# Output projection of the mixer as seven block products, its inputs as blocks and sums of blocks, the result read back for the query projection

## The chip, the cores and the metric

One Trainium2 chip, one of its cores. A core has a matrix engine (PE, with its weight loads PEld), a vector engine (DVE), an activation engine (ACT), GpSimd (POOL) and SyncE (SP); each works through its own list of instructions in order. Transfers between DRAM and SBUF are issued here by SP and, for the caches of the decode rows, by POOL. The metric is the time of one execution in microseconds, the median of three runs.

## The reference

One step of a one-layer decoder on 512 prompt tokens and 8 decode tokens, 520 columns in all, with a model width of 2048. Cut to what matters here:

```python
y = jnp.concatenate([y_rnn, y_ml], axis=-1).astype(h.dtype) @ w['w_out']   # mixer
x = x + y.astype(x.dtype)
q = (rmsnorm(x, w['g_xattn']) @ w['w_cq'])                                 # cross attention
...
x = x + o @ w['w_co']
x = x + (jnp.square(jax.nn.relu(hf @ w['w_up'])) @ w['w_down'])
```

The product with `w_out` is 2048 x 2048 by 2048 x 520. Its inputs come from two head groups: rows 0 to 1023 of `y` from the RG-LRU group after a norm over all of them, rows 1024 to 2047 from the mLSTM group, each gated by a sigmoid of a column block of `z`.

## The kernel before

Activations lie transposed: a tile has 128 rows of the model width and 520 columns, in two halves of 260. Every float32 product is made of three: a value is cast to a shorter "hi" part (ACT) and the rest is "lo" (DVE), and hi·hi, hi·lo and lo·hi are summed in PSUM. So each matmul takes one 128 x 128 block of weights and 260 columns.

All weight products are a list of jobs, one for each 512 KB of weights (8 blocks of 128 x 128). `run_jobs` issues, for each job, the loads of weights three and four jobs ahead, and the cast and the subtraction of the weights two jobs ahead (`w_split`, L128 and L129; rings of three buffers for `wraw`, `whi` and `wlo`), then a step of every background task (generators in `tasks`), then the job's matmuls, then its `post`, which evicts PSUM. The jobs from the tenth to the middle of the query projection are put in order by the framework's scheduler, by priority and dependencies; the order of what follows is the order of the code.

The stages that the change touches:

- The gate columns of `w_in`, eight products of two jobs each (`ev_og`, L778 to L780): eviction with a scale (DVE), sigmoid (ACT), product (DVE), then a split into `ymh` and `yml` (L230, L231). Beside them the last RG-LRU blocks are scaled (L768) and split into `yrh`, `yrl`. PSUM has two `mm` tiles, so the eviction of one product frees the tile for the product after next.
- `w_out` (`residual`): 16 output blocks, each a plain product of two jobs and 96 matmuls at L202. The residual input comes from `xT` into `xr`; L803 adds it; the sum `x1` is stored to the DRAM tile `dx` (L804) for the later `w_co` stage and at once split into `xah`, `xal` (L233, L234) for the query projection; its squares are summed in `ssx` (L264, L265).
- `w_cq`: 16 products of `xatt` (the splits), with the root of `ssx` applied at the eviction.
- The caches of the decode rows stream through a pool `kv` of 14 tiles of 512 columns, loaded by POOL: one tile for each half of K or V of one decode row, and one for the query or probability rows.

Further on the kernel has the seven-product form already: `quad_jobs` (L1253 for its matmuls) takes a 2 x 2 arrangement of weight blocks A11, A12, A21, A22 and seven products P1 to P7 of 24 matmuls each; four combinations of weights (S3, S1, S2 and S2's successor) are made on DVE at L1223. The activations come as eight blocks, of which 1, 2 and 3 are plain halves and 4 to 7 are differences. The up projection uses it for 31 of 32 column groups and the down projection for all. Before the up projection the differences for six of the eight pairs of rows go through DRAM (`td`) and two are kept (`fact_out`, `sums_out`, `fact_sums`), while the first column group is a plain product (`up_plain`).

Of the kernel before, what the change touches and what calls it, by code (L numbers as in the profile page):

```python
# [17 lines left out]
P = 128  # L18
# [27 lines left out]
def tile_trunk(ctx: ExitStack, tc: tile.TileContext, a, o):  # L46
# [27 lines left out]
    def stream(shape):  # L74
        return small.tile(list(shape), F32, tag="kv", name=nm("kv"), bufs=14)
# [232 lines left out]
    xact, y = [], []  # L308
# [213 lines left out]
    def ml_decode(h, q, k, hh):  # L522
# [28 lines left out]
        def fetch(b2):  # L551
            qb, ct = [], []
            for b in (2 * b2, 2 * b2 + 1):
                t = stream((P, 512))
                stream_load(t, rows_of(dqk, b * 512, 512))
                qb.append(t)
            for j in range(2):
                t = slot("ct", (P, 2, 256))
                stream_load(t, a["C0"][h, j, :, 2 * b2:2 * b2 + 2])
                ct.append(t)  # L560
            return qb, ct

        ahead = [fetch(0), fetch(1)]
        for b2 in range(NB // 2):
            yield
            qb, ct = ahead.pop(0)
            if b2 + 2 < NB // 2:
                ahead.append(fetch(b2 + 2))
            for j in range(2):
                for i in range(2):  # L570
                    b = 2 * b2 + i
                    c = ct[j][:, i]
                    S.activation(c, c, AF.Copy, scale=bc[:, h, 0, b:b + 1])
                    V.scalar_tensor_tensor(out=c, in0=qb[i][:, 256:512], scalar=gv[:, j, b:b + 1],
                                           in1=c, op0=ALU.mult, op1=ALU.add)
                    junk = sm("junk", (P, 256), 1)
                    V.tensor_tensor_reduce(out=junk, in0=c, in1=qb[i][:, 0:256], op0=ALU.mult,
                                           op1=ALU.add, scale=1.0, scalar=0.0,
                                           accum_out=numd[:, j, b:b + 1])
                load(o["s_C"][h, j, :, 2 * b2:2 * b2 + 2], ct[j])  # L580
# [138 lines left out]
    def rnn(i, xc):  # L719
# [41 lines left out]
        if i == 7:  # L761
# [3 lines left out]
            for i in range(8):  # L765
# [4 lines left out]
                y.append(split(hg[i], "yr"))  # L770


    ym = []

    def ev_og(i):
        def ev(ps):
# [39 lines left out]
    xatt, oact = [], []  # L816
# [32 lines left out]
    def attn_decode_all():  # L849
# [4 lines left out]
        got, scs, dps, pbs = [], {}, {}, {}  # L854

        def fetch(n):
# [3 lines left out]
            ts = [stream((P, 512)) for _ in range(2)]  # L860
            for i in range(2):
                if kind == "K":
                    stream_load(ts[i], a["K"][h, b, i])
                else:
                    stream_load(ts[i].rearrange("p (a b) -> p a b", a=2), a["V"][h, b, i])
            if kind == "K":
                t = stream((P, 512))
                stream_load(t, rows_of(dq_[h], b * 512, 512))
            elif b % 2 == 0:
                t = stream((P, 2, NMEM))  # L870
                stream_load(t, rows_of(dps[h], b * NMEM, 2 * NMEM).rearrange("p (a b) -> p a b", a=2))
                pbs[h] = t
            else:
                t = pbs[h]
# [5 lines left out]
        for n, (kind, h, b) in enumerate(order):  # L880
# [9 lines left out]
            if kind == "K":  # L890
                if b == 0:
                    scs[h] = sm("sc", (P, 2, NB))
                for i in range(2):
                    V.tensor_tensor_reduce(out=ts[i], in0=ts[i], in1=row, op0=ALU.mult, op1=ALU.add,
# [3 lines left out]
            else:  # L898
                for j in range(4):
                    t = ts[j // 2][:, (j % 2) * NMEM:(j % 2 + 1) * NMEM]  # L900
                    V.tensor_tensor_reduce(out=t, in0=t, in1=row[:, b % 2], op0=ALU.mult, op1=ALU.add,
# [222 lines left out]
    def pair_slot(name):  # L1124
        return slot(name, (P, 2, HT), F32R)

    def split_to(out, src, g=None):

        hi, lo = out[:, 0], out[:, 1]
        if g is None:  # L1130
            S.copy(hi, src)
            V.tensor_tensor(out=lo, in0=src, in1=hi.bitcast(F32), op=ALU.subtract)
        else:
            S.activation(hi, src, AF.Copy, scale=g)
            V.scalar_tensor_tensor(out=lo, in0=src, scalar=g, in1=hi.bitcast(F32),
                                   op0=ALU.mult, op1=ALU.subtract)

# [7 lines left out]
    NKEPT = 2  # L1145
# [5 lines left out]
    def fact_out(x1, n):  # L1151
# [10 lines left out]
        if kp:  # L1162
            S.activation(r[:, 2:4], halves(x1), AF.Copy, scale=pc(C_FFN, n))
            block_sums(r)
            if i < len(td):
                start(sums_out(tkept.pop(i), i))
        else:
# [12 lines left out]
    def fact_sums():  # L1180

        n = len(td)
        for i in range(KB // 2):
            tact[i][1], tact[i][2], tact[i][3] = fact[2 * i][0], fact[2 * i + 1][0], fact[2 * i + 1][1]

        def fetch(j, some):
            for i in some:
                tact[i][j] = pair_slot("ta")
                load(tact[i][j].bitcast(F32), td[i][j - 4])
        for i in range(n, KB // 2):  # L1190
            fetch(6, range((i - n) * n // NKEPT, (i - n + 1) * n // NKEPT))
            for j in (6, 4, 5, 7):
                tact[i][j] = pair_slot("ta")
                split_to(tact[i][j], tkept[i][:, j])
            del tkept[i]
            yield
        for j in (4, 5, 7):
            fetch(j, range(n // 2))
            yield
            fetch(j, range(n // 2, n))  # L1200
            yield

    def quad_jobs(srcs, acts, nacc, evac, order=None):
# [4 lines left out]
        def raw2(name, src=None):  # L1208
            t = late["sb"].tile([P, 8, P], F32, tag="wq", name=nm(name), bufs=5)
# [30 lines left out]
        def mm(p, wh, wl):  # L1240
            acc = ACC[p]
            if acc not in ps:
                ps[acc] = mm_tile()
# [40 lines left out]

    def up_plain(i):
# [3 lines left out]
        def mm(mp, kp, wh, wl):  # L1289
            if kp == 0:  # L1290
                box["ps"] = mm_tile()
            ps = box["ps"]
            for j in range(8):
                x = fact[2 * j + kp]
                for wi, (w, b) in enumerate(((wh, 0), (wh, 1), (wl, 0))):
                    for hf in range(2):
                        PE.matmul(ps[:, hf, 0:HT], w[:, j, :], x[hf][:, b],  # L1297
                                  start=(kp == 0 and j == 0 and wi == 0), stop=(kp == 1 and j == 7 and wi == 2))

        def post(mp):  # L1300
# [3 lines left out]
            for hf in range(2):  # L1304
                blk = (1 - hf, 2 + hf)[mp]
                V.scalar_tensor_tensor(out=r[:, blk], in0=box["ps"][:, hf, 0:HT], scalar=0.0,
                                       in1=st["rssf"][:, HALF[hf]], op0=ALU.max, op1=ALU.mult)
            if mp:
                start(hidden(r, i))

        js = []
        for mp in range(2):
            for kp in range(2):
                js.append(dict(src=a["w_up"][i, mp, kp], mm=lambda wh, wl, mp=mp, kp=kp: mm(mp, kp, wh, wl)))
            js[-1]["post"] = lambda mp=mp: post(mp)
        return js

# [163 lines left out]
    jobs += residual("w_co", oact, dx[0], dx[1], "ssf", fact_out, lambda: start(fact_sums(), 2.0))  # L1481
# [34 lines left out]
def _pack(i):  # L1516
# [10 lines left out]
    for base, name in ((C_MIX, "g_mix"), (C_X, "g_xattn"), (C_FFN, "g_ffn"), (C_FIN, "g_final"),  # L1527
# [33 lines left out]
        w_out=gran(i["w_out"][0]), w_cq=gran(i["w_cq"][0]), w_co=gran(i["w_co"][0]),  # L1561
# [50 lines left out]
```

## Time and profile before

| what | value |
|---|---|
| median of three runs | 2691.73 us (2691.72 to 2692.03) |
| the profiled execution's own time | 2690.68 us |
| its span from first to last instruction | 2688.8 us |
| busy: PE, DVE, ACT, POOL | 2663.4, 2053.1, 1220.3, 152.0 us |
| PE in the `w_out` stage, 589 to 772 us | busy 183.0 of 183.0 us |
| DVE and ACT in the same stretch | busy 70.3 and 52.1 us |

The span is what the trace covers; the execution's own time has 1.9 us more around it. Engine times are busy times. Matmuls overlap, so the mean duration of one is not its cost: the cost is the distance between their starts.

### The profile page before, as it was taken

What the parts mean: (1) busy time and instruction counts of PE and PEld (TensorE: products, weight loads), DVE (VectorE), ACT (ScalarE), POOL (GpSimd) and SP (SyncE); (2) the same over time, 40 slices, a digit from 0 to 9 for tenths busy, and PEclk for the clock granted to TensorE, in tenths of its full rate; (3) what the DMA queues carried; (4) which work ended last, traced back from release to release, by engine and by line L of the source; (5) the groups of instructions that cost most, each with busy time, mean ns of one, the idle gap of its engine ahead of it and who ended that gap; (6) DMA issues with size and microseconds to landing.
All of it is one profiled execution on the core that took longest, in us unless ns stands there. A gap on an engine that the chain in (4) does not pass through costs nothing.

```text
span 2688.8 us, 52718 instructions
## 1 busy us (share of the span) xinstructions
PE 2663.4 (99%) x21586; PEld 2628.4 (98%) x21586; DVE 2053.1 (76%) x3447; ACT 1220.3 (45%) x1653; POOL 152.0 (6%) x288
## 2 busy tenths in 40 slices
PE   9999999999999999999999999999999999999997
PEld 9999999999999998989999999999999999999997
DVE  6786686853345567775469999999999898898898
ACT  5646355542233135444345555555554333333344
POOL 0011010000001322210000000000000000000001
PEclk9999999999999999999999999999999999999999
DMA  5354353524436787876566656556569666555642
GB/s 203 105 189 138 119 168 105 170 95 139 138 126 200 261 271 259 276 249 195 184 213 218 218 190 211 192 192 211 191 223 336 233 215 225 170 165 206 206 134 88
DMA packets 225923, 512.41 MB, mean 191 GB/s; under 512 B 25502, under 2 KB 91710, under 8 KB 225682
## 3 DMA queue, kind: packets, MB, share of 16 engines
q1 hardware_dynamic: 205074, 441.92, 49.3%
q0 software_dynamic: 20608, 67.13, 7.6%
q8 instruction: 170, 2.79, 0.4%
q14 instruction: 71, 0.58, 0.1%
HBM read 416.16 MB, written 92.94 MB: 189 GB/s over the span
## 4 chain that ended last, share of the span: by engine, by line
PE 92%; issue 4%; DVE 2%; DMA 1%; ACT 1%; POOL 0%; SPq 0%; POOLq 0%; DVEq 0%; ACTq 0%
PE mm L1253 44%; PE mm L202 35%; PE mm L982 3%; PE mm L1013 3%; PE aux L221 3%; PE mm L1297 1%; DMA out_rh<-hs 1%; DVE wlo L129 0%; PE aux L729 0%; PE aux L658 0%; DMA wraw<-in_w_in 0%; PE aux L662 0%; ACT whi L128 0%; DMA wraw<-in_w_mv 0%; PE aux L655 0%
## 5 line engine op out<-in xcount | busy, mean ns | idle before, releaser
L128 ACT CAST whi<-wraw 128x1024 fp32r<-128x1024 f32 x396 | 416.0, 1050 | 810.0 <-PE mm L1253 369.8
L1253 PE MATMUL mm<-ha,whi 128*128 128x260 f32 x3584 | 644.3, 283 | 1.5 <-ACT whi L128 1.0
L129 DVE TENSOR_TENSOR wlo<-wraw,whi 128x1024 fp32r<-128x1024 f32 x396 | 484.1, 1222 | 203.4 <-ACT whi L128 201.4
L1253 PEld LDWEIGHTS mm<-ha,whi 128*128 128x128 f32 x3584 | 551.4, 188 | 2.4 <-ACT whi L128 1.2
L1253 PE MATMUL mm<-ha,wlo 128*128 128x260 f32 x1792 | 505.4, 282 | 0.5 <-DVE wlo L129 0.5
L1253 PE MATMUL mm<-ta,whi 128*128 128x260 f32 x1984 | 358.4, 282 | 0.0
L1253 PEld LDWEIGHTS mm<-ha,wlo 128*128 128x128 f32 x1792 | 337.0, 188 | 1.0 <-DVE wlo L129 0.9
L1253 PEld LDWEIGHTS mm<-ta,whi 128*128 128x128 f32 x1984 | 305.4, 188 | 0.0
L1253 PE MATMUL mm<-ta,wlo 128*128 128x260 f32 x992 | 279.9, 282 | 0.0
L1253 PE MATMUL mm<-fa,whi 128*128 128x260 f32 x1488 | 270.9, 283 | 0.0
L202 PE MATMUL mm<-xh,whi 128*128 128x260 f32 x1280 | 263.9, 287 | 0.0
L202 PE MATMUL mm<-xl,whi 128*128 128x260 f32 x1280 | 259.4, 283 | 0.0
L202 PE MATMUL mm<-xh,wlo 128*128 128x260 f32 x1280 | 257.2, 282 | 0.0
L1253 PEld LDWEIGHTS mm<-fa,whi 128*128 128x128 f32 x1488 | 229.2, 188 | 0.0
L137 ACT CAST whi<-wraw 128x1024 fp32r<-128x1024 f32 x100 | 105.0, 1050 | 251.8 <-PE mm L202 92.4
L128 ACT CAST whi<-A 128x1024 fp32r<-128x1024 f32 x126 | 132.2, 1049 | 187.2 <-PE mm L1253 133.5
L1253 PE MATMUL mm<-fa,wlo 128*128 128x260 f32 x744 | 210.2, 283 | 0.0
L1362 DVE TENSOR_TENSOR X<-mm,X 128x260 f32<-128x260 f32 x448 | 170.9, 422 | 41.0 <-PE mm L1253 40.1
L202 PEld LDWEIGHTS mm<-xh,whi 128*128 128x128 f32 x1280 | 198.2, 188 | 1.2
L202 PEld LDWEIGHTS mm<-xh,wlo 128*128 128x128 f32 x1280 | 198.0, 189 | 0.2
L202 PEld LDWEIGHTS mm<-xl,whi 128*128 128x128 f32 x1280 | 197.7, 189 | 0.3
L1253 PEld LDWEIGHTS mm<-ta,wlo 128*128 128x128 f32 x992 | 186.9, 188 | 0.0
(397 smaller groups left out, 5246.5 us busy)
## 6 DMA issues: line engine op xcount, KB each, us to landing
ha<-hc SPq DMA_DIRECT2D x224, 260.0 KB, 5.3
wraw<-in_w_in SPq DMA_DIRECT2D x80, 512.0 KB, 4.2
wraw<-in_w_up SPq DMA_DIRECT2D x66, 512.0 KB, 5.6
wraw<-in_w_down SPq DMA_DIRECT2D x64, 512.0 KB, 4.2
A<-in_w_down SPq DMA_DIRECT2D x64, 512.0 KB, 5.6
A<-in_w_up SPq DMA_DIRECT2D x62, 512.0 KB, 5.7
hc<-hhi SPq DMA_DIRECT2D x32, 910.0 KB, 4.3
hc<-r SPq DMA_DIRECT2D x32, 910.0 KB
```

The costliest lines, as they stand in the source:

```text
L128: S.copy(hi, raw)
L129: V.tensor_tensor(out=lo, in0=raw, in1=hi.bitcast(F32), op=ALU.subtract)
L137: S.copy(hi, raw)
L202: PE.matmul(ps[:, hf, 0:HT], w[:, j, :], x[:, HALF[hf]], start=(k == 0 and wi == 0), stop=(k == n - 1 and wi == 2))
L221: PE.matmul(out, u, v, start=first and i == 0, stop=last and i == 2)
L982: PE.matmul(box["ps"], w[:, i, :], x, start=(k == 0 and wi == 0), stop=(k == KB - 1 and wi == 2))
L1013: PE.matmul(box["ps"][:, i], x[:, ms], w[:, j], start=(k == 0 and wi == 0), stop=(k == KB - 1 and wi == 2))
L1253: PE.matmul(out, w[:, j, :], x[:, b], start=(new and k == 0 and wi == 0), stop=(p == LAST[acc] and k == per - 1 and wi == 2), skip_group_c ...
L1297: PE.matmul(ps[:, hf, 0:HT], w[:, j, :], x[hf][:, b], start=(kp == 0 and j == 0 and wi == 0), stop=(kp == 1 and j == 7 and wi == 2))
L1362: V.tensor_tensor(out=x, in0=c, in1=x, op=ALU.add)
```

## The change

`w_out` becomes one plain group of two output blocks (`out_plain`, four jobs, 192 matmuls) and seven groups of seven products (`out_quad`, 49 jobs, 168 matmuls a group), by the same `quad_jobs` as further on, with its weights in the `kv` pool and its partial sums in `mm` and `aux` tiles of PSUM. Its inputs are split in halves (`y_out`), and for each pair of rows four differences are made on DVE (`y_sums`); six pairs go to DRAM as hi and lo and come back as 24 tiles `ta` (`block_loads`), two pairs are kept. Inputs and differences hold so many of the 66 `slots` that `x1` is no longer split as it is made: blocks 0 to 13 are stored to `dx` and, during the last group, read back and split (`x1_again`); blocks 14 and 15 are split directly. The `kv` pool becomes 7 tiles of 1024 columns, and each transfer of the decode caches has twice the size. `w_out` is laid out in blocks in the input array.

```diff
     def stream(shape):
-        return small.tile(list(shape), F32, tag="kv", name=nm("kv"), bufs=14)
+        return small.tile(list(shape), F32, tag="kv", name=nm("kv"), bufs=7)
...
-                y.append(split(hg[i], "yr"))
+                y_out(hg[i], i)
...
-            ym.append(split(hm[i], "ym"))
+            y_out(hm[i], 8 + i)
             if i == 7:
-                assert not tasks and len(y) == 8
-                y.extend(ym)
+                start(block_loads(ty, fy, ydram, ykept), 2.0)
...
+    def y_out(t, n):
+        fy[n] = [pair_slot("fy") for _ in range(2)]
+        for hf in range(2):
+            split_to(fy[n][hf], t[:, HALF[hf]])
+        if n % 2 == 0:
+            y_even[n // 2] = t
+        else:
+            start(y_sums(n // 2, y_even.pop(n // 2), t))
+
+    def y_sums(i, t0, t1):
+        yield
+        r = stream((P, 4, HT))
+        b12, b11, b21, b22 = t0[:, HALF[1]], t0[:, HALF[0]], t1[:, HALF[0]], t1[:, HALF[1]]
+        for k, p, q in ((0, b12, b11), (2, b22, r[:, 0]), (1, b22, b12), (3, b21, r[:, 2])):
+            V.tensor_tensor(out=r[:, k], in0=p, in1=q, op=ALU.subtract)
+        if i >= len(ydram):
+            ykept[i] = {j: r[:, j - 4] for j in range(4, 8)}
+            return
+        yield
+        hi = small.tile([P, 4, HT], F32R, tag="kv", name=nm("kv"), bufs=7)
+        S.copy(hi, r)
+        V.tensor_tensor(out=r.bitcast(F32R), in0=r, in1=hi.bitcast(F32), op=ALU.subtract)
+        for b, x in enumerate((hi.bitcast(F32), r)):
+            load(ydram[i][:, :, b].rearrange("j p c -> p j c"), x)
...
+    def x1_load(m):
+        for n in (2 * m, 2 * m + 1):
+            x1[n] = slot("x1") if m else xr_tile()
+            load(x1[n], a["xT"][n])
+
+    def x1_done(n):
+        load(dx[0][n], x1[n])
...
+        add_sq(st["ssx"], x1[n], n == 0)
...
+        if n >= KB - 2:
+            xatt[n] = split(x1[n], "xa", pc(C_X, n))
+
+    def x1_again():
+        raw = {}
+        for n in range(0, KB, 2):
+            for k in (n, n + 1):
+                if k < KB - 2:
+                    raw[k] = slot("x1")
+                    load(raw[k], dx[0][k])
+            if n:
+                for k in (n - 2, n - 1):
+                    xatt[k] = split(raw.pop(k), "xa", pc(C_X, k))
+            yield
+
+    def out_plain():
+        def post(mp, ps):
+            V.tensor_tensor(out=halves(x1[mp]), in0=ps[:, :, 0:HT], in1=halves(x1[mp]), op=ALU.add)
+            x1_done(mp)
+            if mp:
+                x1_load(1)
+        js = plain_pair(a["w_out"][0], fy, post)
+        js[0]["pre"] = lambda: x1_load(0)
+        js[1], js[2] = js[2], js[1]
         return js
+
+    def out_quad(m):
+        def evac(p, ps):
+            n, hf = dict(P1=(0, 0), P2=(0, 0), P6=(0, 1), P5=(1, 1), P7=(1, 1), P3=(0, 1), P4=(1, 0))[p]
+            x = x1[2 * m + n][:, HALF[hf]]
+            V.tensor_tensor(out=x, in0=ps[:, 0, 0:HT], in1=x, op=ALU.add)
+            if p == "P5" and m + 1 < KB // 2:
+                x1_load(m + 1)
+            if p in ("P3", "P4"):
+                x1_done(2 * m + n)
+            if p == "P4" and m == KB // 2 - 2:
+                start(x1_again())
...
-    jobs += residual("w_out", y, [a["xT"][n] for n in range(KB)], dx[0], "ssx",
-                     lambda x1, n: xatt.append(split(x1, "xa", pc(C_X, n))))
+    jobs += out_plain()
+    for m in range(1, KB // 2):
+        jobs += out_quad(m)
```

`block_loads` is the old `fact_sums` with its arguments passed in, and waits until a kept pair is there; `plain_pair` is the body of the old `up_plain`; `quad_jobs` gets `early=True`, which takes the tiles of weights from `kv` and the partial sums y and z from `aux`.

In the compiled program PE's list is the same before and after the `w_out` stage, but for line numbers. Three places where the lists change follow. First DVE, in the gate products: the rows around the eviction of the fifth of the eight products (`og_6877<-mm_6764` before, `og_6905<-mm_6773` now; `wlo` are weights two jobs ahead, `kv_6847` and `kv_6852` the differences of two pairs of rows). Before:

```order
L129 TENSOR_TENSOR wlo_6888<-wraw_6748,whi_6887 128x1024
L231 TENSOR_TENSOR yml_6745<-hh_2792,ymh_6744 128x520
L231 TENSOR_TENSOR yrl_6756<-hs_4509,yrh_6755 128x520
L231 TENSOR_TENSOR yrl_6761<-hs_4975,yrh_6760 128x520
L231 TENSOR_TENSOR yrl_6821<-hs_5933,yrh_6820 128x520
L231 TENSOR_TENSOR yrl_6826<-hs_6392,yrh_6825 128x520
L778 TENSOR_TENSOR og_6877<-mm_6764,rssq_722 128x520
```

and now:

```order
L819 TENSOR_TENSOR kv_6847<-hs_3541,hs_3083 128x260
L819 TENSOR_TENSOR kv_6847<-hs_3541,kv_6847 128x260
L819 TENSOR_TENSOR kv_6852<-hh_2789 128x260
L819 TENSOR_TENSOR kv_6852<-hh_2790,hh_2789 128x260
L798 TENSOR_TENSOR fy_6830<-hs_5915,fy_6830 128x260
L798 TENSOR_TENSOR fy_6836<-hs_6368,fy_6836 128x260
L819 TENSOR_TENSOR kv_6852<-hh_2790,kv_6852 128x260
L130 TENSOR_TENSOR wlo_6988<-wraw_6822,whi_6987 128x1024
L798 TENSOR_TENSOR fy_6837<-hs_6368,fy_6837 128x260
L819 TENSOR_TENSOR kv_6852<-hh_2790,kv_6852 128x260
L826 TENSOR_TENSOR kv_6847<-kv_6847,kv_6921 128x1040
L775 TENSOR_TENSOR og_6905<-mm_6773,rssq_728 128x520
```

Between the last sum of the RG-LRU squares (`ssr`) and this eviction DVE's list had 43 rows and now has 73: one `wlo` more (7 for 6), 22 subtractions of 128x260 for the splits in the place of 11 of 128x520, 15 differences of 128x260 and 3 subtractions of 128x1040; the other rows are the same.

Second SP, where the plain group ends and the first group of seven begins. Before, the residual input of a block (`xr`) was loaded two blocks ahead of its use, behind the store of an earlier block:

```order
L804 DMA dx_0_103<-x_1008_7348 128x520
L797 DMA xr_7483<-in_xT 128x520
L107 DMA wraw_7413<-in_w_out 128x1024
L107 DMA wraw_7477<-in_w_out 128x1024
L804 DMA dx_1_104<-x_1019_7467 128x520
L797 DMA xr_7604<-in_xT 128x520
```

and now the inputs of blocks 2 and 3 (`x_1045`, `x_1046`) stand behind the store of block 1:

```order
L839 DMA ta_7550<-yd_108 128x520
L839 DMA ta_7552<-yd_103 128x520
L839 DMA ta_7554<-yd_104 128x520
L839 DMA ta_7556<-yd_105 128x520
L1364 DMA dx_1_110<-xr_7321 128x520
L1361 DMA x_1045_7611<-in_xT 128x520
L1361 DMA x_1046_7613<-in_xT 128x520
L839 DMA ta_7621<-yd_106 128x520
```

The store of `dx_1` waits for the eviction of the plain group's last job, and the first eviction of the next group adds into `x_1045`.

Third SP again, where the last group (`x_1195` and `x_1196` are its two blocks) meets the query projection. Before:

```order
L804 DMA dx_13_116<-x_1163_8919 128x520
L797 DMA xr_9056<-in_xT 128x520
L107 DMA wraw_8986<-in_w_cq 128x1024
L107 DMA wraw_9050<-in_w_cq 128x1024
L804 DMA dx_14_117<-x_1175_9040 128x520
L107 DMA wraw_9107<-in_w_cq 128x1024
L107 DMA wraw_9173<-in_w_cq 128x1024
L804 DMA dx_15_118<-x_1187_9161 128x520
```

and now, the last part of the reads from `dx`:

```order
L108 DMA wraw_9214<-in_w_cq 128x1024
L1380 DMA x_1241_9177<-dx_8_117 128x520
L1380 DMA x_1242_9179<-dx_9_118 128x520
L1380 DMA x_1250_9220<-dx_10_119 128x520
L1380 DMA x_1251_9222<-dx_11_120 128x520
L108 DMA wraw_9265<-in_w_cq 128x1024
L1364 DMA dx_14_123<-x_1195_8906 128x520
L108 DMA wraw_9318<-in_w_cq 128x1024
L1380 DMA x_1262_9271<-dx_12_121 128x520
L1364 DMA dx_15_124<-x_1196_8908 128x520
L1380 DMA x_1263_9273<-dx_13_122 128x520
```

Reads and loads of weights alternate; the reads of blocks 12 and 13 come last, each behind a row that waits for DVE.

More of the change, by code (lines that the diff above doesn't have):

```diff
@@ L307, in tile_trunk @@
     st = {}
[L308 removed]
+    xact = []
     uc = [[] for _ in range(4)]
@@ L1166, in fact_out @@
                 start(sums_out(tkept.pop(i), i))
+            else:
+                tkept[i] = {j: r[:, j] for j in range(4, 8)}
         else:
```

173 lines of the change are left out of this document (93 added, 80 removed).

## The prediction

> **What bounds the kernel now.** I read the page first, then the chain of work that ended last, then PE's waits, then windows by stage. The page's busy shares, in microseconds:
>
> ```profile
> span 2688.8 us, 52718 instructions
> PE 2663.4 (99%) x21586; PEld 2628.4 (98%) x21586; DVE 2053.1 (76%) x3447; ACT 1220.3 (45%) x1653; POOL 152.0 (6%) x288
> ```
>
> PE is the bound, but a share is an average. The chain in order of time (start, length, what) shows the stage:
>
> ```profile
> 531.89 247.06 PE mm L202 x2064
> 778.95 0.88 PE aux L253 x4
> ```
>
> This one piece is five gate products (480 matmuls), the whole `w_out` stage (1536) and the first job of the query projection (48): 2064 matmuls with no step to another engine. One costs 247.06 / 2064 = 0.1197 us; here nothing but the number of matmuls sets the time. The same view has the seven-product form in the later stages:
>
> ```profile
> 1401.77 632.60 PE mm L1253 x5279
> ```
>
> 632.60 / 5279 = 0.1198 us: a matmul of that form costs the same. What PE waited for elsewhere (engine, tile, line; sum, times, longest):
>
> ```profile
> PE aux L729 <- DVE C L666: 3.2, 1, 3.2
> PE aux L655 <- ACT g L730: 1.4, 1, 1.4
> ```
>
> These lie ahead of the stage. By windows (length; busy PE, PEld, DVE, ACT, POOL; granted clock; DMA share, GB/s):
>
> ```profile
> 521.00:560.70 39.70, 39.70 (x327) 39.46 (x326) 32.44 (x48) 26.16 (x34) 0.00 (x0) 1.00 0.31 94
> 589.00:772.00 183.00, 183.00 (x1533) 183.00 (x1532) 70.34 (x79) 52.09 (x64) 0.00 (x0) 1.00 0.43 134
> 1330.00:2000.00 670.00, 670.00 (x5590) 669.88 (x5589) 587.32 (x746) 359.10 (x435) 0.00 (x0) 1.00 0.60 204
> ```
>
> In the `w_out` stage DVE is 38% busy and DMA 43%, so there is room. Just before it, in the gate products, DVE is 82% busy (32.44 of 39.70). In the up projection, which has the form already, DVE is 88% busy and PE still never stops.
>
> **What is removed.** 1536 matmuls become 192 + 7 x 168 = 1368, so 168 go: 168 x 0.1197 = 20.1 us, all on the chain.
>
> **What DVE and ACT do in the groups of seven.** Prices (count, busy, mean ns; idle before):
>
> ```profile
> L129 DVE TENSOR_TENSOR wlo<-wraw,whi 128x1024 fp32r<-128x1024 f32 x396 | 484.1, 1222 | 203.4 <-ACT whi L128 201.4
> L1362 DVE TENSOR_TENSOR X<-mm,X 128x260 f32<-128x260 f32 x448 | 170.9, 422 | 41.0 <-PE mm L1253 40.1
> L265 DVE TENSOR_TENSOR ssx<-ssx,sq 128x520 f32<-128x520 f32 x12 | 8.3, 694 | 0.0
> L234 DVE SCALAR_TENSOR_TENSOR xal<-x,par,xah 128x520 fp32r<-128x520 f32 x13 | 9.8, 755 | 0.0
> L233 ACT ACTIVATE xah<-x,par 128x520 fp32r<-128x520 f32 x13 | 9.5, 727 | 0.0
> ```
>
> A group has 7 weight subtractions and 4 combinations of weights at 1.22 us, 7 evictions at 0.42 and 2 sums at 0.69: 13.4 + 3.0 + 1.4 = 17.8 us, against 168 x 0.1197 = 20.1 us of PE. It fits with the same margin as in the up projection, so I cost it at nothing; the cover is the 2.3 us left in each group.
>
> **The gate products: a late eviction.** The differences are made while DVE is busiest. Timeline of DVE, then of ACT, before the change (start, length; in brackets the idle time before it):
>
> ```profile
> 560.00 0.70 DVE L778 TENSOR_TENSOR og<-mm,rssq 128x520 f32<-128x520 f32 x1
> ```
>
> ```profile
> 566.24 1.05 ACT L128 CAST whi<-wraw 128x1024 fp32r<-128x1024 f32 x1 [2.18 <-PE mm L202]
> ```
>
> The first row is the eviction of the fifth gate product, the second follows the end of the sixth, when the seventh starts and needs that PSUM tile: 566.24 - 560.70 = 5.5 us to spare. Ahead of this eviction DVE now has 73 rows for 43: 1 weight subtraction more (1.2), 22 of 128x260 for 11 of 128x520 (22 x 0.42 - 11 x 0.69 = 1.7), 15 differences (6.3) and 3 subtractions of 128x1040 (3.7, by the length of L129): 12.9 us. Neighbouring starts on the timeline lie some 0.08 us closer than durations say, which takes 2.5 off: 10.4. DVE's idle time in that window, 39.70 - 32.44 = 7.3 us, takes up part. If it takes all, nothing is lost (10.4 - 7.3 = 3.1, under 5.5); if none, 12.9 - 5.5 = 7.4 us. That idle time is mostly waiting for ACT, which has more casts ahead of it too, so I let DVE fill about half: 10.4 - 3.7 = 6.7 us later, which is 6.7 - 5.5 = **1.2 us** too late, the value taken, with 0 and 7.4 as bounds. Queued behind that eviction are the weights of the later jobs, but those are two jobs ahead. From 560.7 on DVE was lightly loaded, so nothing later is late.
>
> **The first group: a late input.** The rows for SP issues and landings (of DMA issues: count, KB, median us to landing):
>
> ```profile
> 601.73 0.33 SPq L804 DMA_DIRECT2D dx<-x  x1
> 602.11 0.43 SPq L797 DMA_DIRECT2D xr<-in_xT  x1
> ```
>
> ```profile
> ta<-td SPq DMA_DIRECT2D x24, 260.0 KB, 6.0
> X<-dx SPq DMA_DIRECT2D x16, 260.0 KB, 3.8
> dx<-x SPq DMA_DIRECT2D x32, 260.0 KB, 2.1
> ```
>
> `x_1045` is loaded behind the store of `dx_1`, which waits for the eviction of the plain group (0.7 us after its end): issued about 0.7 + 0.4 + 0.4 = 1.5 us into the group, landed 3.8 to 6.0 us later, added 0.4 us after: 5.7 to 7.9. P6 accumulates into the tile that this eviction reads, and could start at 48 x 0.1197 = 5.7. Behind the waiting eviction on DVE stand only weights for P7 and later, due 11.5 us in. Bounds 0 to 2.2 us; I take **1.0 us**, the middle. Later groups ask for this input at P5 of the group before, 8 us earlier.
>
> **The handover to the query projection.** Fourteen blocks are read back and split within the last group: 14 x 0.755 = 10.6 us on DVE and 14 x 0.727 = 10.2 us on ACT more. DVE has 17.8 + 10.6 = 28.4 us to do in 20.1. Yet block k is due only with the (6k)th matmul of the projection, block 13 at 20.1 + 78 x 0.1197 + 0.9 (the sums of `ssx` on PE, above) = 30.3 us. The reads start when the store of block 13 is issued, 0.4 us into the group; the last, of block 13, stands on SP behind the store of block 15, at about 20.1 + 0.4 + DVE's backlog of 2 = 22.5. With 3.8 to 6.0 us to landing and 1.5 for the split it is ready at 27.8 to 30.0, in time. If a weight load ahead of it holds SP for one more subtraction or two, it comes up to 2.5 us late. Bounds 0 to 3, **0.4 us** taken, near the lower end because the sum meets the deadline.
>
> **Transfers of the caches.** The same bytes in half as many issues. In 1000 to 1300 us PE loses 1.7 us now:
>
> ```profile
> 1000.00:1300.00 300.00, 298.31 (x2095) 277.52 (x2094) 207.06 (x495) 136.88 (x239) 51.86 (x96) 1.00 0.72 239
> ```
>
> So at most 1.7 to gain, and about as much to lose; I take 0. Four rows ahead need at most seven of the seven tiles.
>
> **A rule on the clock.** The longest wait of PE above, 3.2 us, lies in a window with the clock at 1.00:
>
> ```profile
> 200.00:300.00 100.00, 96.15 (x774) 94.29 (x773) 74.50 (x179) 53.86 (x89) 8.58 (x16) 1.00 0.41 135
> ```
>
> So by this trace a wait of up to 3.2 us costs only itself. The Trainium skill, "TensorE: Matmul & The Clock Gate", section "What's actually happening", says that after an idle window of about 3.4 us the matrix engine runs at half its clock until it has been busy for about as long. By that rule a wait longer than this would cost an estimated 1.7 us more; of the three waits only the first, at its upper bound, is that long, and none at the value taken. No run shown here has such a wait in mid-program.
>
> **The sum.** -20.1 + 1.2 + 1.0 + 0.4 = -17.5 us. On the profiled execution: 2690.68 - 17.5 = 2673.2 (span 2688.8 - 17.5 = 2671.3). Its time is 1.05 us under the median, so the median after is 2691.73 - 17.5 = **2674.2 us**.
>
> **The rivals.**
> - No wait appears: DVE's idle time takes the extra work, the input lands in 3.8 us. Then -20.1: 2671.6 us. For it: in the trace the same form starts at 1401.77 with no wait. Against: there no differences are made beside gate products. Chance 0.17.
> - The gate products wait at their bound: 7.4 for 1.2, so 2680.4 us; with a wait of that length the clock could add something. For it: DVE's idle time there is ACT's doing. Chance 0.13.
> - Slower: the reads gate the evictions in the last group. Splits stand between evictions on DVE's list. If every pair of reads could only be issued after the eviction of one product, because its tile comes free then, a product takes 2 x 0.43 + 3.8 + 0.73 + 0.76 + 0.42 = 6.6 us and not 2.9: 7 x 3.7 = 26 us. For 0.4 that gives 2674.2 + 25.6 = 2699.8 us. It decides from the point where a read is issued less than its landing time ahead of the eviction behind it. Against: each product frees the eight tiles of its block, where a pair asks for six (two to read into, four for the splits). Chance 0.05.
> - No change: DVE paces the groups. It needs 20.1 / 7 = 2.9 us more a group than PE, so 23.0 us on DVE for my 17.8, 29% above rows that hold in the up projection. 2691.7 us, chance 0.04.
> - The change doesn't save what it says: PE's compiled list has the 1368 matmuls, and the rate of that form is 0.1198 us. Under 0.01.
>
> **How the numbers follow.** My forecast has 0.60, the rivals 0.17, 0.13, 0.05 and 0.04. The range runs from the case without waits, less 0.6 us for the caches (2671.0), to all upper bounds together, 2671.6 + 7.4 + 2.2 + 3 = 2684.2, so 2684.0. Outside lie the last rivals. A run tells about 0.2%, 5.4 us, from no change. Faster: 0.60 + 0.17 + 0.13 + part of the rest = 0.91; same 0.04; slower 0.05.
>
> **What would show it.** Right: a piece of the chain from the gate products to the query projection that holds about 1896 matmuls, PE waits of 1 to 2 us at an eviction of `mm` by line 775 and at the first eviction into `x1`, and DVE near 88% from 612 to 755 us. Wrong: PE below 95% busy in the groups, DVE waiting for reads of `dx`, a clock below 1.00 after 540 us, or new PE waits between 900 and 1300 us.

## The result, and the profile after

The changed kernel takes 2668.53 us, the median of 4 runs (2667.73 to 2670.34), against 2691.72 us (2691.40 to 2692.03): a ratio of 0.9915, with a 95% interval from 0.9898 to 0.9932. The forecast was 2674.2 us with a range from 2671.0. The direction and the main term were right; the kernel gained more than the lowest value that the prediction allowed.

The first part of the page of after (span; busy time of each engine):

```profile
span 2667.0 us, 52574 instructions
PE 2639.8 (99%) x21418; PEld 2602.9 (98%) x21418; DVE 2135.2 (80%) x3593; ACT 1253.2 (47%) x1704; POOL 108.3 (4%) x184
```

The profiled execution takes 2668.74 us, 21.94 less than that of before. The chain of after in order of time (start, length, what), from the late gate eviction to the query projection:

```profile
560.38 1.53 DVE kv L819 x5
...
564.91 1.15 DVE kv L826
566.06 0.62 DVE og L775
566.82 23.27 PE mm L203 x192
590.09 22.96 PE mm L1329 x192
613.05 2.88 PE mm L1286 x24
...
750.99 2.86 PE mm L1286 x24
753.86 5.77 PE mm L203 x48
```

The chain leaves PE once, for the differences and subtractions of the block sums on DVE (L819, L826) and the eviction behind them (L775). From 566.82 it stays on PE. `w_out`, from the start of its first matmul at 589.93 to the first of the query projection, takes 163.77 us for 192 + 7 x 168 = 1368 matmuls, 0.1197 us each. No other wait of PE is left there; the view of PE's waits from 520 to 780 us has one row:

```profile
PE mm L203 <- DVE og L775: 0.9, 1, 0.9
```

By windows, the gate products and the groups of after (same columns as before):

```profile
521.00:560.70 39.70, 39.70 (x327) 39.46 (x326) 36.58 (x67) 28.86 (x44) 0.00 (x0) 1.00 0.45 144
...
612.00:755.00 143.00, 143.00 (x1196) 142.98 (x1195) 118.80 (x147) 67.43 (x76) 0.73 (x1) 1.00 0.55 184
```

DVE goes from 32.44 to 36.58 us busy in the first window, so it loses 4.1 of its 7.3 us of idle time (the prediction let it lose 3.7). In the groups it is busy for 118.80 of 143 us, 83%, where 88% was forecast.

To see where the rest came from, I took from the traces the start of the first matmul of each stage. Lengths of the stages in us (from `w_out` to the query products; from these to the first key product; the attention part with the products of the memory; `w_co`; up; down):

| kernel | w_out | query | attention | w_co | up | down |
|---|---|---|---|---|---|---|
| before | 183.69 | 187.59 | 226.05 | 191.11 | 647.96 | 649.78 |
| after | 163.77 | 187.59 | 228.90 | 189.05 | 644.68 | 649.43 |

`w_out` starts at 589.32 before and 589.93 after; the sum of the changes up to the last matmul is 0.61 - 19.92 + 0 + 2.85 - 2.06 - 3.28 - 0.35 = -22.15 us. The stage that was changed gives -19.92, of which the gate's wait takes 1.10 back. The other terms, -5.34 in `w_co` and up, -0.35 in down and +2.85 in the attention part, lie in stages whose lists of instructions on PE, DVE and ACT did not change, but for the layout of the `kv` tiles and their loads in the attention part. The experiments ask whether the change caused them.

### The profile page after: what moved, and what is told of

It is laid out like the page before. It is cut to its first block, busy times and chain, and to the rows that moved or that the text cites. A ratio compares the mean times of both kernels' runs of the same rounds, so it can differ in the third digit from the quotient of the medians.

```text
span 2667.0 us, 52574 instructions
## 1 busy us (share of the span) xinstructions
PE 2639.8 (99%) x21418; PEld 2602.9 (98%) x21418; DVE 2135.2 (80%) x3593; ACT 1253.2 (47%) x1704; POOL 108.3 (4%) x184
## 4 chain that ended last, share of the span: by engine, by line
PE 91%; issue 4%; DVE 2%; DMA 2%; ACT 1%; POOL 0%; SPq 0%; POOLq 0%; DVEq 0%; ACTq 0%
PE mm L1286 46%; PE mm L203 29%; PE mm L1050 3%; PE mm L1081 3%; PE aux L222 3%; PE aux L1286 2%; PE mm L1329 2%; DVE wlo L130 1%; PE aux L657 1%; DMA wraw<-in_w_in 1%; PE aux L728 0%; PE aux L661 0%; DMA hc<-r 0%; PE aux L654 0%; DMA wraw<-in_w_mv 0%
## 5 line engine op out<-in xcount | busy, mean ns | idle before, releaser
L1286 PE MATMUL mm<-ta,whi 128*128 128x260 f32 x2320 | 419.3, 283 | 0.0
L1286 PEld LDWEIGHTS mm<-ta,whi 128*128 128x128 f32 x2320 | 356.2, 188 | 0.0
L1286 PE MATMUL mm<-ta,wlo 128*128 128x260 f32 x1160 | 326.8, 282 | 0.0
L1286 PEld LDWEIGHTS mm<-ta,wlo 128*128 128x128 f32 x1160 | 218.4, 188 | 0.0
```

What stands on the lines that cost most here:

```text
L1286: PE.matmul(out, w[:, j, :], x[:, b], start=(new and k == 0 and wi == 0), stop=(p == LAST[acc] and k == per - 1 and wi == 2), skip_group_c ...
```

## The experiments

Theory P for the -5.34 us: the matmuls' mean spacing depends on which of the 66 slots their activations lie in, and the change, which takes tiles from the ring in another order, moved them. Rival C: it is the position of PE's code, which is 168 matmuls shorter ahead of these stages. Rival N: chance of the execution. In the up stage the spacing from start to start is 119.83 ns before and 119.21 ns after, in every stretch of 100 us alike.

**One unused tile in the kernel before.**

```diff
     with tc.manual_schedule():
+        G.memset(slot("pad"), 0.0)
         run_jobs(n_cq, n_early + 2, True)
```

> The kernel before, with one unused tile taken from the ring of 66 slots ahead of the query projection (a memset on POOL writes it). Every engine's list is the same but for that memset; 48% of the matmuls of the up projection read their activations from another slot, weights and PSUM tiles stay where they were. Theory P (the mean spacing of the matmuls is set by which slots their activations lie in): in the w_co and up stages (1216 to 2038 us) the mean spacing moves by 0.2 to 1 ns from the 120.0 and 119.83 ns of before, in either direction, which is 1 to 5 us over 5376 matmuls of the up stage, while the stages ahead of the query projection keep theirs within 0.1 ns. Rival C (position of PE's code) and rival N (chance of the execution): C gives 119.83 again and 2691.7 us; N gives values that vary from run to run of one kernel.

**The code moved, the slots not.**

```diff
-        for _ in range(14):
+        for _ in range(20):
             PE.matmul(warm[:, 0:P], ones, ones, start=True, stop=True)
```

> The kernel before with 6 more warm-up matmuls at its start (20 for 14), so that PE's code of every later stage lies elsewhere by 12 instructions and every address of an operand is that of before. Theory P: the same spacing as before in every stage (120.0 in w_co, 119.83 ns in the up stage), total 2691.7 plus at most the 2.5 us of the matmuls. Rival C (the place of the code sets the spacing): another mean, off by 0.2 ns or more.

**The kernel after again.** No edit.

> The kernel after, unchanged. Theories P and C: the same spacings as in its first profile (119.21 ns in the up stage against 119.83 of before), PE waits 0.9 us for the gate's eviction again, total 2668.5. Rival N (chance of the execution): the up stage comes out between 119.2 and 119.8 ns, and the gain outside the changed stage (2.5 us) moves by a microsecond or more.

One window of each, 1500 to 1900 us, all of it in the up stage (the number behind PE's busy time counts its matmuls, with some three at the edges that are only partly inside). Before:

```profile
1500.00:1900.00 400.00, 400.00 (x3341) 400.00 (x3340) 365.76 (x458) 219.56 (x259) 0.00 (x0) 1.00 0.59 197
```

Before, with more warm-up matmuls:

```profile
1500.00:1900.00 400.00, 400.00 (x3340) 400.00 (x3339) 366.57 (x460) 219.42 (x258) 0.00 (x0) 1.00 0.59 197
```

Before, with one unused tile:

```profile
1500.00:1900.00 400.00, 400.00 (x3348) 400.00 (x3347) 367.39 (x460) 219.51 (x259) 0.00 (x0) 1.00 0.59 198
```

After:

```profile
1500.00:1900.00 400.00, 400.00 (x3358) 400.00 (x3357) 366.60 (x460) 220.75 (x260) 0.00 (x0) 1.00 0.59 199
```

PE is 100% busy at a granted clock of 1.00 in all four, and yet it gets through 3341, 3340, 3348 and 3358 matmuls. Moving the code leaves 119.83 ns; one unused tile gives 119.56 ns, `w_co` of 190.55 and up of 646.66 us, 0.56 and 1.30 us less than before; after gives 189.07 and 644.68 again. Rival N falls, and C as far as a shift of 12 instructions can tell. The compiled programs say more: for each of the 5208 matmuls in the groups of the up stage, before and after have the weights and the partial sum at the same address, and the activations at another. So of PE's operands only the place of the activations differs. That it makes the whole of the -5.34 us follows from this and from what one tile does; no run put the activations of after back into the slots of before. The times agree as far as they reach: 2690.34 us, a ratio of 0.9989 (0.998 to 0.9999), with the tile; 2693.59, 1.0003 (0.9994 to 1.0013), with the code moved; 2669.05, 0.9909 (0.9893 to 0.9926), for after.

**One unused tile in the kernel after, and two in the kernel before.** The same edit in after, and `for _ in range(2):` ahead of the memset in before.

> The kernel after with one unused tile taken from the ring of slots ahead of the query projection, as in the kernel before with the same edit. Every list is the same but for one memset on POOL; half of PE's operands lie in other slots from there on. Theory P: the mean spacing in w_co and the up stage moves off 119.45 and 119.21 ns by 0.1 to 0.6 ns, in either direction (0.5 to 3 us over the up stage); the stages ahead keep theirs. Rival (the gain belongs to the changed code, not to the slots): 119.21 ns as in both profiles of after.

> The kernel before with two unused tiles taken from the ring of slots ahead of the query projection, not one. Theory P: a third mean spacing in the up stage, other than 119.83 (none) and 119.56 ns (one), between 119.0 and 120.2, repeated to 0.02 ns within the stage. Rival (one pad's effect was the memset on POOL or chance): 119.56 or 119.83 again. It also gives one more sample of the attention part with the old transfers.

After with the tile: 119.48 ns, `w_co` 189.56 and up 646.11 us; so after loses 0.5 and 1.4 us of its gain by a tile that nobody uses. The total, 2670.85 us (2669.02 to 2676.62), is too coarse for that. Before with two tiles: 119.56 ns, the value of one tile and not a third one, as expected of P, although the two layouts have only half of their operands in the same slots; `w_co` 190.42, up 646.56 us, total 2690.16 us, 0.9992 (0.9983 to 1.0001). So theory P missed its number here and the rival's came out; its reason (the memset, or chance) does not fit, since the spacings of the single positions in the group differ between the two kernels by 2.4 ns on average, and only their mean is the same.

**The cache transfers alone, in the kernel before.** The ring of 14 tiles of 512 columns becomes one of 7 tiles of 1024, each with one transfer.

```diff
-        return small.tile(list(shape), F32, tag="kv", name=nm("kv"), bufs=14)
+        return small.tile(list(shape), F32, tag="kv", name=nm("kv"), bufs=7)
...
-            ts = [stream((P, 512)) for _ in range(2)]
-            for i in range(2):
-                if kind == "K":
-                    stream_load(ts[i], a["K"][h, b, i])
+            ts = stream((P, 2, 512))
+                stream_load(ts, a["K"][h, b].rearrange("i p c -> p i c"))
```

> The kernel before with the cache transfers of the change alone (7 tiles of 1024 columns for 14 of 512). PE's list and all addresses of PE's operands are those of before. Theory P: spacing in the up stage 119.83 ns as before. Theory K (the larger transfers are what costs the attention part its 2.9 us): the stretch from the first key product to w_co gets 2 to 3 us longer and the total 2691.7 + 2 to 3 = about 2694. Rival: the attention part loses by other means, and the total stays at 2691.7 within 0.5.

**The same ring as after, transfers of the old size.**

```diff
-                stream_load(ts, a["K"][h, b].rearrange("i p c -> p i c"))
+                for i in range(2):
+                    stream_load(ts[:, i], a["K"][h, b, i])
```

and the same for `V`, `dq`, `dp` and `dqk`.

> The kernel after with every cache transfer of 1024 columns issued as two of 512, into the same seven tiles, so the sizes and the number of issues are those of before and the tiles those of after. All of PE's operands lie where they lie in after. Theory K1 (larger transfers cost the attention part 2 us): the stretch from 961 to 1187 us (of before's times) is 1 to 2.5 us shorter than in after, and the total about 2667.5. Theory K2 (the coarser ring of seven tiles costs it): no change, 2668.5 to 2669. Rival (chance of the execution): the stretch lies anywhere in the 3 us that repeats of one kernel show.

The attention part lasts 230.59 us with the new transfers in before, and 231.01 us with the old size in the ring of after. Spacing in the up stage stays at 119.83 and 119.21 ns. All traces of this study together: 226.05, 227.76, 227.58 and 227.01 us with the old ring (mean 227.10), and 230.59, 228.90, 228.50, 231.01, 228.44, 230.11, 232.22, 231.24, 226.95 and 228.12 us with the new one (mean 229.61; in the longest the clock was halved there for 3.4 us). So a single profile can't price it, but the two groups lie 2.5 us apart, with some 0.7 us of standard error. Theory K1, the size of the transfers, is contradicted: it expected a part 1 to 2.5 us shorter than in after and a total of about 2667.5, and all five runs took 2671.25 us or more. K2, the coarser ring, remains and isn't shown: its total, 2668.5 to 2669, was missed as well, and why the old size is some 4 us slower in the new ring is open. The time of the transfers alone, 2694.59 us, a ratio of 1.0003 (0.9994 to 1.0012), allows -1.6 to +3.2 us. After with transfers of the old size takes 2673.22 us (2671.25 to 2677.47), 0.9935 (0.9922 to 0.9947).

**The gate's wait: leave out the subtractions ahead of it.**

```diff
         S.copy(hi, r)
-        V.tensor_tensor(out=r.bitcast(F32R), in0=r, in1=hi.bitcast(F32), op=ALU.subtract)
```

> The kernel after, leaving out the subtraction of line 826 (six of 128x1040, 1.15 us each on the chain), so that the lo parts of the stored block sums are the sums themselves. Three of the six stand ahead of the late gate eviction, so it comes 3.5 us earlier. Theory G (DVE's list ahead of the eviction makes PE wait, with no idle time on DVE from 554 to 567 us): the wait of 0.9 us is gone, and the stretch from 531 us to the start of w_out is 1.2 us shorter. Rival (it is ACT's casts or the transfers of weights): the wait stays at 0.5 to 0.9 us. The up stage's spacing may move by theory P.

The chain of this kernel, gate products and start of `w_out`:

```profile
534.00 57.59 PE mm L203 x480
591.60 22.95 PE mm L1328 x192
```

The piece of PE runs through; the wait is gone. From the first of these matmuls to the first of `w_out` it takes 57.43 us, as before the change; after needs 58.53. So the late eviction costs 1.10 us, and DVE's list is its cause. The total, 2670.34 us (0.9918; 0.9903 to 0.9933), does not show it: up is 646.54 us, at 119.56 ns a matmul, since slots come free in another order again (in the compiled program 21% of the activations of the up stage's groups lie elsewhere than in after).

**The gate's wait: the differences on POOL.**

```diff
-            V.tensor_tensor(out=r[:, k], in0=p, in1=q, op=ALU.subtract)
+            (G if i < 6 else V).tensor_tensor(out=r[:, k], in0=p, in1=q, op=ALU.subtract)
```

> The kernel after with the 24 differences of the six stored pairs (line 819) on POOL instead of DVE; ahead of the late gate eviction DVE has 19 rows less, 15 differences and one subtraction among them, so some 7 us. Theory G (DVE's list ahead of the eviction makes PE wait): the 0.9 us wait of PE at the gate eviction is gone, w_out starts 1.2 us earlier against the stretch from 531 us, the total falls by about 1. Rival (ACT's casts, not DVE, set when DVE gets to the eviction): the wait stays at 0.5 to 0.9 us. A third way: the differences at about 0.73 us each on POOL make the blocks late, and a wait appears in the first group of seven, 1 to 5 us. By theory P the up stage's spacing may move off 119.21 ns, since slots come free in another order.

It got worse: 2676.43 us, 0.9933 (0.9918 to 0.9948), and none of the three ways expected is what happened. PE's waits in the stage:

```profile
PE mm L203 <- DVE og L775: 4.3, 1, 4.3
```

The two timelines of this kernel show where the time goes. DVE:

```profile
538.94 1.24 DVE L767 SCALAR_TENSOR_TENSOR hs<-hs,par,rr 128x520 f32<-128x520 f32 x1
...
557.93 0.69 DVE L775 TENSOR_TENSOR og<-mm,rssq 128x520 f32<-128x520 f32 x1
...
566.96 0.70 DVE L775 TENSOR_TENSOR og<-mm,rssq 128x520 f32<-128x520 f32 x1 [2.07 <-POOL kv L819]
```

POOL:

```profile
538.54 1.09 POOL L819 TENSOR_TENSOR kv<-hs,kv 128x260 f32<-128x260 f32 x1
539.59 1.21 POOL L819 TENSOR_TENSOR kv<-hs,hs 128x260 f32<-128x260 f32 x1
```

In after the same kind of scaling takes DVE 0.75 us, and the eviction of the fourth gate product comes at 552.74:

```profile
546.99 0.75 DVE L767 SCALAR_TENSOR_TENSOR hs<-hs,par,rr 128x520 f32<-128x520 f32 x1
...
552.74 0.69 DVE L775 TENSOR_TENSOR og<-mm,rssq 128x520 f32<-128x520 f32 x1
```

While both run, each slows: DVE's scaling takes 1.24 for 0.75 us, POOL's difference 1.09 to 1.21 us, and once 3.64, for the 0.74 of its shortest. PE's wait of 4.3 us ends at 558.76, behind the fourth eviction (557.93), so it is one product earlier than the late one of after. DVE's rows from 538.94 to 547.8 take some 3.6 us longer than the same rows undisturbed (an estimate from five rows), and that delay stands ahead of this eviction. The fifth, at 566.96, waits 2.07 us for POOL, but PE does not wait for it. From the first gate matmul of this stretch to `w_out` it takes 63.49 us for after's 58.53; in the wait's wake the granted clock is halved for 3.4 us. The Trainium skill, "SBUF — State Buffer", section "Who interferes with whom", says that a DVE instruction with two inputs in SBUF contends with a GpSimd instruction that reads SBUF; these rows agree.

**The handover without its cover.** All reads behind the last store.

```diff
-            if p == "P4" and m == KB // 2 - 2:
-                start(x1_again())
+            if p == "P4" and m == KB // 2 - 1:
+                start(x1_again(), 9.0)
```

> The kernel after with all the reads of dx for the query projection behind the last store of dx, after the last group instead of within it. It shows what the cover of the last group is worth. By the prediction's terms: the first block needs 0.4 + 3.8 to 6.0 us for its read and 1.5 for its split, then each block takes 0.76 us on DVE against 0.72 us of PE for its 6 matmuls: PE waits 5.7 to 7.9 us for the first block and about 1 more for the rest, so the time from the last group to the second query product grows by 6 to 10 us. Rival (the reads are no cost in either place, because the wait for the sums of squares, about 8 us, is there anyway): under 2 us. By theory P the spacing of w_co and of the up stage moves as well, by up to 0.6 ns.

PE's waits of this kernel from 745 to 800 us, then its chain there, then the window from 745 to 775 us:

```profile
PE mm L203 <- ACT xah L234: 6.6, 1, 6.6
```

```profile
753.87 4.33 DMA x<-dx
...
758.22 0.74 ACT xah L234
...
759.00 7.93 PE mm L203 x48
```

```profile
745.00:775.00 30.00, 23.44 (x177) 22.83 (x176) 19.98 (x29) 20.93 (x27) 0.00 (x0) 0.89 0.60 211
```

The first read lands 4.33 us after its issue, PE waits 6.6 us, and then the first job of the query projection takes 7.93 us for 5.77, with the granted clock at 0.89 on average in this window. `w_out` and the query stage are 6.81 and 2.23 us longer than in after, 9.0 together: 6.6 of waiting and 2.2 in that first job. The wait is the size that was expected; the 2.2 us come with the lower clock, where about 1 us of waiting for the other blocks was expected. The total is 2680.09 us, 0.9948 (0.9931 to 0.9964). So within the last group the reads are hidden, worth 9 us.

**More work for DVE in the groups.**

```diff
             V.tensor_tensor(out=x, in0=ps[:, 0, 0:HT], in1=x, op=ALU.add)
+            if "jk" not in st:
+                st["jk"] = slot("jk")
+                V.memset(st["jk"], 0.0)
+            V.tensor_tensor(out=st["jk"], in0=st["jk"], in1=st["jk"], op=ALU.add)
```

> The kernel after with one more 128x520 addition on DVE (0.69 us, on a tile of zeros that nothing else uses) behind each eviction of the seven groups: 7 x 0.69 = 4.8 us a group, 34 us in all. By the prediction's cover (17.8 us of DVE in 20.1 of PE) DVE would need 22.6 us a group and PE would wait 2.5 us in each of seven: +17 us. By the window of after (DVE 190.53 of 228 us busy, so 3.3 us free in 20.1) it is 1.5 x 7 = +10.5 us. Rival (DVE was never near the limit, because neighbouring instructions overlap): under +2 us.

Its window over the groups, then PE's waits from 745 to 800 us and the window from 745 to 775 us:

```profile
612.00:755.00 143.00, 143.00 (x1197) 142.98 (x1196) 140.78 (x189) 62.82 (x69) 0.73 (x1) 1.00 0.51 171
```

```profile
PE aux L254 <- DVE ssx L266: 5.5, 1, 5.5
PE mm L203 <- ACT xah L234: 0.7, 1, 0.7
PE mm L203 <- DVE xal L235: 0.5, 2, 0.3
```

```profile
745.00:775.00 30.00, 23.27 (x167) 21.93 (x166) 23.40 (x35) 19.98 (x27) 0.00 (x0) 0.83 0.58 195
```

DVE is busy for 140.78 of 143 us, 98%, and PE doesn't lose a matmul: `w_out` lasts 163.75 us. So both prices of the cover (+17 and +10.5 us) were wrong: they put waits of PE into the groups, and there are none. The first did not count that neighbouring DVE instructions overlap: 7 additions and 20 other rows at 0.08 us take 2.2 us off the 22.6, which leaves 20.4 for 20.1 us of PE. The bill comes at the end, where the splits of the last group are added: the sums of squares are 5.5 us late, and the query stage takes 197.40 for 187.59 us. Of these 9.8 us 6.7 are waits of PE; behind them the granted clock falls, to 0.83 on average in the last window. The total is 2678.38 us, 0.9939 (0.9925 to 0.9954). That it comes near the lower price is chance, since the cost lies in another stage.

**The first group's input later.**

```diff
             if mp:
+                for n in range(2):
+                    load(slot("dm"), a["xT"][n])
                 x1_load(1)
```

> The kernel after with two loads of 260 KB into unused tiles issued ahead of the two residual inputs of the first group of seven, so that these are issued 0.86 us later and land 1 to 2 us later. In after they were issued at 614.19, the eviction that adds them ran at 618.13 when DVE came to it, and P6, which needs its PSUM tile, started at 618.81: 0.26 us to spare. By the prediction's third term PE then waits 0.5 to 1.5 us in the first group. Rival (nothing there waits for that input): no wait, w_out as long as in after within 0.2 us.

After has, on DVE's timeline in the first group, the eviction right behind a weight subtraction:

```profile
616.99 1.23 DVE L130 TENSOR_TENSOR wlo<-kv,whi 128x1024 fp32r<-128x1024 f32 x1
618.13 0.42 DVE L1401 TENSOR_TENSOR x<-mm,x 128x260 f32<-128x260 f32 x1
```

With the later input DVE waits for it:

```profile
621.04 0.43 DVE L1403 TENSOR_TENSOR x<-mm,x 128x260 f32<-128x260 f32 x1 [1.25 <-DMA x<-in_xT]
```

PE then loses 0.36 us in the first group, less than the 0.5 to 1.5 expected, and 0.58 us in all of `w_out` (164.35 us); the total is 2671.78 us, 0.9925 (0.9911 to 0.9938). The two unused tiles also move later slots: the query stage is 0.59 us longer without a wait, so only the 0.36 us can be put down to the input. So in after this input was just in time: the mechanism is there, and its price starts about a microsecond later.

## Why the prediction came out high

- **The 168 matmuls: -20.1 forecast, -19.92 measured** for `w_out` from start to start. Right, at 0.1196 us a matmul before and 0.1197 after.
- **The gate's late eviction: +1.2 forecast, +1.10 measured**, and shown by leaving out work ahead of it. Right, with the split of DVE's idle time about as assumed. Its upper bound was too high by its own working: 7.4 is 12.9 - 5.5 and leaves out the 2.5 us of overlap taken off just before, with which it is 4.9. And the sign of being right, a piece of the chain with about 1896 matmuls, could not come together with this wait, which cuts the piece.
- **The first group's input: +1.0 forecast, none found.** The step took 3.8 to 6.0 us to landing; the loads issued at 614.19 had landed by 618.13, when DVE came to them. A delay of 0.86 us at issue brought a wait of 0.36. The mechanism was right; the middle of the bounds was too high.
- **The handover: +0.4 forecast, 0.00 measured**: the query stage takes 187.59 us in both kernels. The deadline was met, as its sum said. Without the cover it costs 9 us, within the 6 to 10 expected, though 2.2 of them by the clock and not by the blocks.
- **DVE in the groups: nothing forecast, nothing measured**, and there is more room than the 2.3 us a group: PE runs through at 98% of DVE.
- **The caches: 0 forecast, with 1.7 either way.** The attention part is longer by 2.85 us in the two profiles and by 2.5 between the means of 4 and 10 traces. The step priced it by the PE idle time of one profiled execution; the four traces with the old ring alone span 1.7 us in this part.
- **The step that failed** is the low end of the range: "the case without waits, less 0.6 us for the caches (2671.0)". It supposes that stages whose lists are unchanged keep their time, so the sum has no term for where the change moves their operands. `w_co` and up became 2.06 and 3.28 us shorter with the same lists at the same granted clock, with nothing of PE's operands in the groups of up moved but the activations. The working took 0.1198 us a matmul in the up stage and looked no further; 0.63 ns less seems small, but over the 5208 matmuls of the up stage's groups it is 3.3 us. What in the addresses does it is open.
- **The clock.** The prediction said that "a wait of up to 3.2 us costs only itself". One execution carried that. In after's own profile the wait at the same place is 3.1 us and the clock does fall (below).

Put together, of the 5.7 us by which the forecast was too high, the two waits that did not come make 1.4; the slots give 5.3 and the attention part takes back some 2.5. The rest is about 1.5, and 1.3 of it is the spread of single executions: the profile of before was 1.05 us under its median, that of after 0.2 us over. Without the -5.3 the time would have been about 2673.9 us, inside the range.

## What to carry to other kernels

A change in one stage can move the time of stages that it doesn't touch, because it changes where the allocator puts their operands; when a saving is below 1% of the span, compare the stages one by one by the starts of their matmuls before crediting the edit, and put an unused tile into the ring to see how much is mere placement. When work is moved into the shadow of a matmul stage, price it by the stage behind: DVE at 98% cost nothing in the groups, and 9.8 us at the handover. An idle engine is no free place either: look at what its instructions share with the busy one.

## What the runs showed of the hardware

**Spacing by slot.** With PE 100% busy at a clock of 1.00, the mean spacing of the same 128 x 260 matmuls lay between 119.17 and 119.83 ns, by the layout. Within one layout each of the 168 positions of a group keeps its own spacing, from 114 to 127 ns, in steps of 0.83 ns, group after group; it is the same to 0.13 ns in before with other code ahead, and in after again, and differs by 2.5 to 2.7 ns on average when half of the slots change. It is no property of a single slot, since positions whose three neighbours on either side keep their slots change too. Yet it is local: after and the kernel without the subtractions share long runs of positions with the same slots, and over two of them, 40 and 30 positions long, the spacings agree to 0.1 ns. What in the addresses does it is open.

**The clock falls after about 3 us of waiting, not always.** After, the wait for the last RG-LRU block and the stretch behind it, by windows:

```profile
247.00:250.62 3.62, 1.14 (x6) 0.99 (x7) 3.62 (x9) 2.16 (x6) 1.08 (x2) 1.00 0.29 78
250.62:254.10 3.48, 3.48 (x19) 3.48 (x18) 3.48 (x12) 3.45 (x6) 0.00 (x0) 0.51 0.61 218
```

Before, the same two stretches:

```profile
248.00:251.70 3.70, 1.14 (x6) 0.99 (x7) 3.70 (x9) 2.15 (x6) 1.07 (x2) 1.00 0.26 69
251.70:255.20 3.50, 3.50 (x31) 3.45 (x29) 3.50 (x12) 3.47 (x6) 0.00 (x0) 1.00 0.67 229
```

After the same gap PE runs 19 matmuls at a clock of 0.51 in one execution and 31 at 1.00 in the other. In the 14 traces the wait there was followed by no fall at 2.6, 2.7, 2.8, 2.9 and twice 3.2 us, and by one of 3.4 or 6.8 us at 2.9, 3.1 (twice), 3.3 (three times), 3.9 and 4.0 us. The 60 matmuls behind the wait took 7.8 us without a fall, 9.4 with one of 3.4 us and 10.5 with one of 6.8 us, so a fall cost some 1.6 or 2.6 us here, which is the size of the spread between runs of one kernel. The Trainium skill, "TensorE: Matmul & The Clock Gate", section "What's actually happening", gives a window of 3413 ns that runs freely, and half the clock after an idle one. The lengths of the falls agree. The length of the wait does not settle it here: where a wait of 2.9 us was followed by a fall, the matmuls on either side start 3.30 us apart, less than that window, and in before they start 3.58 us apart without a fall. It could be a matter of where the window lay, which no run here shows.
